# DeltaNet tasks: order edges behind the latest dense evacuation, scaling or substitution step

## The chip, cores and metric

The kernel runs on one core of one Trainium2 chip. The metric is device time in microseconds (us). The kernel before takes 1623.09 us, the median of 3 runs (1622.53 to 1624.87).

## What is computed

A trunk of two layers over 16 meta tokens and 512 tokens with 1024 channels: a forgetting-attention layer and a gated DeltaNet layer, each followed by a feed-forward block with a short causal convolution (FFN). The change concerns the DeltaNet layer alone. Cut to what matters, with 8 heads of 128 channels and chunks of 64 or 128 rows:

```
proj = h @ w_in                       # q, k, v, output gate, two gate scalars per head
q, k, v = silu(causal_dwconv(q, 4 taps)), ...    # then q and k are l2-normalised
g = cumsum of the log decay, beta = sigmoid(gate)
for each chunk:
    A = strictly lower part of beta * exp(g_i - g_j) * (k_i . k_j)
    T = inverse(I + A)
    u = T @ (beta * v - (beta * exp(g) * k) @ S)
    o = (exp(g) * q) @ S + (masked q k^T) @ u
    S = exp(g_last) * S + k_decayed^T @ u
out = rmsnorm(o) * gate @ w_out
```

## The kernel before

The sequence is worked on in two halves of 272 and 256 columns. The large products are made by `dense`: for one 128-channel tile of one half it issues 24 matmuls into one PSUM tile (`ps`, L339; the activations are split into a high part `xh` and a low part `xl`). The tile is then taken out of PSUM by VectorE (DVE). In the DeltaNet layer there are three such evacuations: `conv_tile` L778 (`ub`, DVE) with a scaling on ScalarE (ACT) at L785 and the remaining taps on DVE at L794; the output gate `og` L1547 (`oz`, DVE) with a tanh on ACT at L1549; and the output projection `part` L914 and L916 (`m`, DVE). Until `ub` or `oz` has been read, TensorE (PE) has no free PSUM tile and stops.

Beside the dense products run generator tasks for four groups (g0 to g3) of two heads each. A planner, the class `Flow`, keeps a clock of its own that advances with each matmul issued; `tick` lets a task take its next step when its wake time has passed, and the `yield` of a step says how long to wait (in us). The tasks that matter here:

- `decays` (L1100 to L1129): loads the decays of a head by DMA into `gcr` (L1114), and makes masked differences on DVE (L1123, tiles `Dm` and `ATQD`).
- `gram_k` (L1132 to L1161): products of keys on PE, their diagonal on DVE (L1144, L1145, tile `y`), a power on GpSimd (POOL, L1146, tile `rk`), then `rho` on DVE (L1147) and what follows from it (L1148 to L1157).
- `solve` (L1271 to L1374): the inverse. POOL does a substitution of 31 steps of two instructions (L1295, L1296) for each group; the result goes out and comes back by DMA into `Rc`; DVE transposes it into `Tc` (L1309); further products follow on PE (L1317 to L1370, tile `l`), with copies on DVE (L1327) and ACT (L1328).
- the meta-token inverse, whose products are L1220 on PE and whose copies are `Y` on DVE (L1245 to L1265), the scan over the chunks (L1380 to L1413 on PE, ACT and DVE: `VB`, `KD`, `U`, `S`), and the heads' output (`MO` with a power on POOL at L1466, `OU` on ACT at L1470, the transposition `t` on PE at L1476, `o` on DVE at L1484).

The order on PE is fixed by tokens that are stamped in the planner's order. On DVE, ACT and POOL there was no such rule: the tile scheduler sets the order of their instructions from its own estimate of when each is ready, and each engine then works strictly through its list. An instruction that waits for a DMA therefore holds all that stand behind it on its engine, an evacuation too.

Of the kernel before, what the change touches and what calls it, by code (L numbers as in the profile page):

```python
# [12 lines left out]
AF = mybir.ActivationFunctionType  # L13
ALU = mybir.AluOpType
# [18 lines left out]
T_GRAM = 4.5  # L33
# [12 lines left out]
T_POW = 2.4  # L46
# [67 lines left out]
def trunk(ctx, tc, h0, wflat, params, out):  # L114
    nc = tc.nc
# [25 lines left out]
    def phase(name):  # L141
        turn.clear()
        turn["kinds"] = KINDS[name]
# [81 lines left out]
    class Flow:  # L225
# [10 lines left out]

        def step(self, t):
            self.busy = True
            try:
                r = next(t["gen"])  # L240
            except StopIteration:
                self.tasks.remove(t)
                r = None
            self.busy = False
            t["cond"] = None
            if callable(r):
                t["cond"] = r
            elif r is not None:
                t["wake"] = self.now + r
# [14 lines left out]
        def until(self, cond):  # L264
            assert not self.busy
            while not cond():
                if not self.ready():
                    self.now += 0.5
                    continue
                t = min(self.ready(), key=lambda t: t["wake"])  # L270
                self.now = max(self.now, t["wake"])
                self.step(t)

    flow = Flow()

# [491 lines left out]
    def conv_tile(u, half, ft, taps, base, stride, pool, carry):  # L767
        n = HALF[half][1]
        c0 = taps - 1
        xh, xl, r = xk(half)  # L770
        ps = dense(u, half, xh, xl)
        with tc.high_priority(offset=300):
            ub = pool.tile([P, 275], F32, name="ub", tag="ub", bufs=3)
            if half == 0:
                nc.gpsimd.memset(ub[:, 0:c0], 0.0)
            else:
                nc.gpsimd.tensor_copy(ub[:, 0:c0], carry.pop(ft)[:, :c0])  # L777
            nc.vector.tensor_tensor(ub[:, c0:c0 + n], ps, r[:, :n], op=ALU.mult)  # L778
            if half == 0:
                c = pool.tile([P, 3], F32, name="cy", tag="cy", bufs=8)  # L780
                nc.gpsimd.tensor_copy(c[:, :c0], ub[:, n:n + c0])  # L781
                carry[ft] = c
            w = [prm[:, base + i * stride + ft:base + i * stride + ft + 1] for i in range(taps)]
            cv = tmp2("cv")[:, :n]
            nc.scalar.activation(cv, ub[:, c0:c0 + n], AF.Identity, scale=w[c0])  # L785
            tap = u - DN0 in DN_TAP
            if tap:
                t0 = tmp("cv0")[:, :n]
                if u - DN0 > 13:
                    nc.gpsimd.tensor_scalar(t0, ub[:, 0:n], w[0], None, op0=ALU.mult)  # L790
                else:
                    nc.scalar.activation(t0, ub[:, 0:n], AF.Copy, scale=w[0])
            for i in range(c0 - 1, 0 if tap else -1, -1):
                nc.vector.scalar_tensor_tensor(cv, ub[:, i:i + n], w[i], cv, op0=ALU.mult, op1=ALU.add)  # L794
            if tap:
                nc.gpsimd.tensor_tensor(cv, cv, t0, op=ALU.add)
        return cv
# [73 lines left out]
    def deltanet(layer, post, pre, wcx):  # L871
# [22 lines left out]
        def part(u, half, j, last):  # L894
            n = NT[half]
            if j == 0 and not last:
                drop(*X[half][:2])
                m[half] = take(half, "m", shape=[P, KT, n])
            if j == 0 and last:

                if half == 0:
                    HALF[0] = (CUT, NT[0])
                ssm[half] = SumSq(half)
            if j == 0:
                OHL[half] = split(half, 4 * last)
                if last:
                    drop(O[half])
            x = OHL[half]
            for sub in range(2):
                mt = 2 * j + sub  # L910
                ps = dense(u, half, lambda k: x[:, 0, k, :], lambda k: x[:, 1, k, :], 0, n, sub)
                mm = m[half][:, mt, :]
                if not last:
                    nc.vector.tensor_copy(mm, ps)  # L914
                    continue
                nc.vector.tensor_tensor(mm, mm, ps, op=ALU.add)  # L916
                ssm[half].add(mm)
                if mt == 4:
                    h[half] = take(half, "h", shape=[P, KT, n])
                    nc.gpsimd.dma_start(h[half][:], hd_[half][:, :, CUT if half == 0 else 0:])  # L920
            if j == 3:
                drop(x)
                if last:
                    boundary(half, m[half], ssm[half], post, pre)
                    drop(m[half])
# [4 lines left out]
        with ExitStack() as cx:  # L930
            flow.on = True
            dn_heads(layer, O, cx, part)
            flow.on = False
        phase("ffn")
        wide(wcx)

    def dn_heads(layer, O, cx, part):
# [108 lines left out]
        def group(g):  # L1046
# [84 lines left out]
            def gram_k(half):  # L1131
                s, n = HALF[half]  # L1132
                cs = slice(CI[half][0], CI[half][-1] + 1)
                w = len(CI[half])
# [3 lines left out]
                y, rk, rho, ab, ub, kd = (col(x) for x in ("y", "rk", "rho", "ab", "ub", "kd"))  # L1138
# [5 lines left out]
                        nc.vector.tensor_tensor_reduce(out=dg, in0=pgs[hl][:, i * 128:i * 128 + cn], in1=ident[:, 0:cn], scale=1.0, scalar=0.0, op0=ALU.mult, op1=ALU.add, accum_out=y[:, c, hl:hl + 1])  # L1144
                nc.vector.tensor_scalar(y[:, cs, :], y[:, cs, :], 0.25, EPS, op0=ALU.mult, op1=ALU.add)  # L1145
                nc.gpsimd.tensor_tensor(rk[:, cs, :], y[:, cs, :], mhalf[:, 0:w * NG].rearrange("p (c x) -> p c x", x=NG), op=ALU.pow)  # L1146
                nc.vector.tensor_tensor(rho[:, cs, :], y[:, cs, :], rk[:, cs, :], op=ALU.mult)  # L1147
                nc.vector.tensor_scalar(rk[:, cs, :], rk[:, cs, :], 0.5, None, op0=ALU.mult)  # L1148
                nc.vector.tensor_tensor(ub[:, cs, :], rk[:, cs, :], COL[:, cs, hs4], op=ALU.mult)
# [2 lines left out]
                for hl in range(NG):  # L1152
                    for i, c in enumerate(CI[half]):
                        cn = CH[c][1]
                        o = pgs[hl][:cn, i * 128:i * 128 + cn]
                        d, a = (st["QD"][:, hl * 4 + c - 1, :], st["AT"][:, hl * 4 + c - 1, :]) if c else (st["Dm"][:, hl, :], padded("N", 0)[hm(hl), hm(hl)])
                        nc.vector.scalar_tensor_tensor(a, o, ab[:cn, c, hl:hl + 1], d, op0=ALU.mult, op1=ALU.mult)  # L1157
                if half == 0:
                    nc.vector.tensor_copy(ub[32:64, 0, 0:1], ub[0:32, 0, 1:2])
                yield T_GRAM + 1.5  # L1160
                held["g"] = False  # L1161


# [106 lines left out]
            def solve():  # L1270
# [21 lines left out]
                for l in range(31):  # L1292
                    a, w = l // 4 + 1, 31 - l
                    t = PR[:, 0:a * w].rearrange("p (j i) -> p j i", i=w)
                    nc.gpsimd.tensor_tensor(t, R3[:, 0:a, l:l + 1].to_broadcast([P, a, w]), A3[:, l:l + 1, l + 1:32].to_broadcast([P, a, w]), op=ALU.mult)  # L1295
                    nc.gpsimd.tensor_tensor(R3[:, 0:a, l + 1:32], R3[:, 0:a, l + 1:32], t, op=ALU.subtract)  # L1296
                    yield T_STEP
                for r in range(4):
                    nc.sync.dma_start(dR[:, :, r, :], RB[32 * r:32 * r + 32, :].rearrange("p (j i) -> p j i", i=32))
# [240 lines left out]
        def og(u, half, hd):  # L1540
            c = slice(CUT if half == 0 else 0, HALF[half][1])
            n = c.stop - c.start
# [1 line left out]
            ps = dense(u, half, xh, xl, c.start, c.stop)  # L1544
            otile(half)
            z = tmp2("oz")[:, :n]
            nc.vector.tensor_tensor(z, ps, r[:, c], op=ALU.mult)  # L1547
            th = tmp2("ot")[:, :n]
            nc.scalar.activation(th, z, AF.Tanh, scale=0.5)  # L1549
            o = O[half][:, hd, c]  # L1550
            w = max(written.get((half, hd), 0) - c.start, 0)
            og_done.add((half, hd))
# [96 lines left out]
```

## Time and profile before

| | |
|---|---|
| median of 3 runs | 1623.09 us (1622.53 to 1624.87) |
| the profiled execution | 1624.94 us |
| its span, first to last instruction | 1623.0 us, mean granted TensorE clock 0.966 |
| DeltaNet stage in the span | about 791 to 1215 us |
| PE busy over the span | 1528.3 us (94%) |
| DVE, ACT, POOL busy | 1144.3, 800.0 and 456.2 us |

PE is the busiest engine. The table by stretches shows for each stretch of the span how long each engine was busy, and as PEclk the granted TensorE clock as a share of full speed (0.5 is the lower of its two levels, 1.2 GHz). The lists of waits name an instruction, what ended its wait, the total of these waits, their number and the longest. In a timeline an instruction stands with its start, its duration, and in brackets the idle time of its engine before it and what ended that.

### The profile page before, as it was taken

What the parts mean: (1) busy time and instruction counts of PE and PEld (TensorE: products, weight loads), DVE (VectorE), ACT (ScalarE), POOL (GpSimd) and SP (SyncE); (2) the same over time, 40 slices, a digit from 0 to 9 for tenths busy, and PEclk for the clock granted to TensorE, in tenths of its full rate; (3) what the DMA queues carried; (4) which work ended last, traced back from release to release, by engine and by line L of the source; (5) the groups of instructions that cost most, each with busy time, mean ns of one, the idle gap of its engine ahead of it and who ended that gap; (6) DMA issues with size and microseconds to landing.
All of it is one profiled execution on the core that took longest, in us unless ns stands there. A gap on an engine that the chain in (4) does not pass through costs nothing.

```text
span 1623.0 us, 32915 instructions
## 1 busy us (share of the span) xinstructions
PE 1528.3 (94%) x12462; PEld 1491.8 (92%) x12462; DVE 1144.3 (71%) x2760; ACT 800.0 (49%) x1849; POOL 456.2 (28%) x949
## 2 busy tenths in 40 slices
PE   8999999999999999999779798989898999999996
PEld 6999999899999999998679787988887999999996
DVE  7888888849964665665878765857477864765764
ACT  6777777735543432444463334545454543433441
POOL 6444443135200100114534555161043100100112
PEclk9999999999999999999799898999998999999998
DMA  5322322421323223222233331222231223323321
GB/s 172 100 80 73 86 73 86 132 79 53 105 84 99 92 81 103 92 83 79 93 108 81 76 83 41 63 72 61 78 113 57 80 84 100 93 90 94 100 68 53
DMA packets 66527, 139.55 MB, mean 86 GB/s; under 512 B 22808, under 2 KB 35512, under 8 KB 65984
## 3 DMA queue, kind: packets, MB, share of 16 engines
q1 hardware_dynamic: 65744, 135.08, 28.0%
q8 instruction: 98, 1.61, 0.4%
q0 software_dynamic: 480, 2.15, 0.4%
q14 instruction: 61, 0.50, 0.1%
q10 hardware_dynamic: 144, 0.22, 0.0%
HBM read 132.06 MB, written 5.36 MB: 85 GB/s over the span
## 4 chain that ended last, share of the span: by engine, by line
PE 74%; DVE 11%; POOL 5%; ACT 4%; DMA 3%; issue 3%; SPq 1%; POOLq 0%; DVEq 0%; ACTq 0%
PE ps L339 64%; POOL PR L1295 2%; POOL RB L1296 2%; DVE bt L438 1%; DVE w L310 1%; DVE h L439 1%; PE av L728 1%; DMA gcr<-gcd 1%; DVE cv L794 1%; PE pt L708 1%; DVE xl L405 1%; ACT w L303 1%; PE sc L676 1%; PE sc L677 1%; PE pt L696 1%
## 5 line engine op out<-in xcount | busy, mean ns | idle before, releaser
L339 PE MATMUL ps<-xh,w 128*128 128x256 f32 (+5 forms) x4928 | 974.6, 292 | 30.6 <-DVE ub L778 19.4
L339 PEld LDWEIGHTS ps<-xh,w 128*128 128x128 f32 (+2 forms) x4928 | 793.8, 192 | 37.7 <-DVE ub L778 21.6
L339 PE MATMUL ps<-xl,w 128*128 128x256 f32 (+5 forms) x2464 | 713.2, 290 | 10.8 <-DVE xl L405 10.8
L339 PEld LDWEIGHTS ps<-xl,w 128*128 128x128 f32 (+2 forms) x2464 | 473.9, 192 | 15.7 <-DVE xl L405 13.9
L303 ACT CAST w<-w 128x1024 fp32r<-128x1024 f32 (+2 forms) x218 | 223.3, 1025 | 158.9 <-PE ps L339 143.3
L310 DVE TENSOR_TENSOR w<-w,w 128x1024 fp32r<-128x1024 f32 (+3 forms) x183 | 221.6, 1211 | 112.1 <-ACT w L303 112.1
L794 DVE SCALAR_TENSOR_TENSOR cv<-ub,prm,cv 128x256 f32<-128x256 f32 (+2 forms) x494 | 241.8, 495 | 40.9 <-ACT cv L785 32.0
L339 PE MATMUL ps<-ah,w 128*128 128x256 f32 (+2 forms) x1408 | 265.0, 284 | 0.0
L339 PEld LDWEIGHTS ps<-ah,w 128*128 128x128 f32 x1408 | 221.5, 188 | 0.0
L339 PE MATMUL ps<-al,w 128*128 128x256 f32 (+2 forms) x704 | 199.1, 283 | 0.0
L785 ACT ACTIVATE cv<-ub,prm 128x256 f32<-128x256 f32 (+2 forms) x224 | 113.3, 510 | 150.8 <-DVE ub L778 150.6
L778 DVE TENSOR_TENSOR ub<-ps,r 128x256 f32<-128x256 f32 (+2 forms) x224 | 95.5, 429 | 86.7 <-PE ps L339 83.6
L380 POOL TENSOR_TENSOR ssq<-ssq,sq 128x256 f32<-128x256 f32 (+2 forms) x98 | 93.1, 954 | 147.5 <-ACT sq L379 145.3
L339 PEld LDWEIGHTS ps<-al,w 128*128 128x128 f32 x704 | 132.5, 188 | 0.0
L781 POOL COPY cy<-ub 128x2 f32<-128x2 f32 (+1 forms) x112 | 35.7, 322 | 295.7 <-DVE ub L778 295.0
L310 POOL TENSOR_TENSOR w<-w,w 128x512 fp32r<-128x512 f32 x70 | 93.6, 1357 | 63.5 <-ACT w L303 44.5
L777 POOL COPY ub<-cy 128x2 f32<-128x2 f32 (+1 forms) x112 | 31.7, 283 | 213.8 <-DVE cv L794 173.0
L816 ACT ACTIVATE gl<-cv 128x272 f32<-128x272 f32 (+2 forms) x88 | 36.7, 418 | 47.9 <-DVE cv L794 47.7
L841 DVE TENSOR_TENSOR m<-m,ps 128x256 f32<-128x256 f32 (+2 forms) x64 | 27.2, 424 | 41.5 <-PE ps L339 41.0
L1295 POOL TENSOR_TENSOR PR<-RB,AB 128x60 f32<-128x60 f32 (+24 forms) x124 | 44.6, 360 | 36.6 <-DMA AB<-dA 28.5
L339 PE MATMUL ps<-ohl,w 128*128 128x260 f32 (+1 forms) x384 | 51.7, 288 | 2.6 <-ACT ohl L887 1.0
L339 PEld LDWEIGHTS ps<-ohl,w 128*128 128x128 f32 x384 | 47.7, 190 | 4.1 <-ACT ohl L887 1.3
(325 smaller groups left out, 2175.3 us busy)
## 6 DMA issues: line engine op xcount, KB each, us to landing
w<-wflat SPq DMA_DIRECT2D x184, 512.0 KB, 3.5
w<-wflat SPq DMA_DIRECT2D x32, 448.0 KB, 3.3
cB<-cdram SPq DMA_DIRECT2D x16, 264.0 KB, 3.3
h<-h SPq DMA_DIRECT2D x8, 272.0 KB, 4.8
cB<-cdram SPq DMA_DIRECT2D x16, 136.0 KB, 3.0
h<-h SPq DMA_DIRECT2D x8, 256.0 KB, 4.7
AB<-dA SPq DMA_DIRECT2D x16, 128.0 KB, 2.9
out<-h SPq DMA_DIRECT2D x16, 128.0 KB, 1.8
```

Of the source, the lines that this page charges most:

```text
L303: nc.scalar.copy(wh, w32)
L310: eng.tensor_tensor(wl[:, c], w32[:, c], wh[:, c].bitcast(F32), op=ALU.subtract)
L339: tok(nc.tensor.matmul(o, w[:, a], r[:, c0:c1], start=(i == 0), stop=(i == tot - 1)))
L380: nc.gpsimd.tensor_tensor(self.acc[:, :n], self.acc[:, :n], sq[:, :n], op=ALU.add)
L777: nc.gpsimd.tensor_copy(ub[:, 0:c0], carry.pop(ft)[:, :c0])
L778: nc.vector.tensor_tensor(ub[:, c0:c0 + n], ps, r[:, :n], op=ALU.mult)
L781: nc.gpsimd.tensor_copy(c[:, :c0], ub[:, n:n + c0])
L785: nc.scalar.activation(cv, ub[:, c0:c0 + n], AF.Identity, scale=w[c0])
L794: nc.vector.scalar_tensor_tensor(cv, ub[:, i:i + n], w[i], cv, op0=ALU.mult, op1=ALU.add)
L816: nc.scalar.activation(g, cv, AF.Gelu_apprx_tanh)
L1295: nc.gpsimd.tensor_tensor(t, R3[:, 0:a, l:l + 1].to_broadcast([P, a, w]), A3[:, l:l + 1, l + 1:32].to_broadcast([P, a, w]), op=ALU.mult)
L1296: nc.gpsimd.tensor_tensor(R3[:, 0:a, l + 1:32], R3[:, 0:a, l + 1:32], t, op=ALU.subtract)
```

## The change

A dictionary `anchors` keeps for DVE, ACT and POOL the latest instruction of a kind: on DVE the latest evacuation (`ub`, `oz` or `m`), on ACT the latest scaling or tanh behind an evacuation, on POOL the latest subtraction of the substitution. Every step of a task is traced under `tc.issue_after(anchor)`, so that its instructions on that engine get an order edge behind that anchor. The edges are orders within an engine and add no instruction; the counts of instructions on each engine are the same. In `gram_k` a `yield T_POW` (2.4 us) is put behind the power, and its last `yield` falls from 6.0 to 3.5 us.

```diff
@@ -236,11 +236,14 @@
 
         def step(self, t):
             self.busy = True
-            try:
-                r = next(t["gen"])
-            except StopIteration:
-                self.tasks.remove(t)
-                r = None
+            with ExitStack() as es:
+                for i in anchors.values():
+                    es.enter_context(tc.issue_after(i))
+                try:
+                    r = next(t["gen"])
+                except StopIteration:
+                    self.tasks.remove(t)
+                    r = None
             self.busy = False
             t["cond"] = None
             if callable(r):
@@ -270,6 +273,14 @@
                 t = min(self.ready(), key=lambda t: t["wake"])
                 self.now = max(self.now, t["wake"])
                 self.step(t)
+
+    anchors = {}
+
+    def anchor(engine, inst):
+        if flow.on:
+            anchors[engine] = inst.ins
 
     flow = Flow()
 
@@ -775,14 +786,14 @@
                 nc.gpsimd.memset(ub[:, 0:c0], 0.0)
             else:
                 nc.gpsimd.tensor_copy(ub[:, 0:c0], carry.pop(ft)[:, :c0])
-            nc.vector.tensor_tensor(ub[:, c0:c0 + n], ps, r[:, :n], op=ALU.mult)
+            anchor("dve", nc.vector.tensor_tensor(ub[:, c0:c0 + n], ps, r[:, :n], op=ALU.mult))
             if half == 0:
                 c = pool.tile([P, 3], F32, name="cy", tag="cy", bufs=8)
                 nc.gpsimd.tensor_copy(c[:, :c0], ub[:, n:n + c0])
                 carry[ft] = c
             w = [prm[:, base + i * stride + ft:base + i * stride + ft + 1] for i in range(taps)]
             cv = tmp2("cv")[:, :n]
-            nc.scalar.activation(cv, ub[:, c0:c0 + n], AF.Identity, scale=w[c0])
+            anchor("act", nc.scalar.activation(cv, ub[:, c0:c0 + n], AF.Identity, scale=w[c0]))
             tap = u - DN0 in DN_TAP
             if tap:
                 t0 = tmp("cv0")[:, :n]
@@ -911,9 +922,9 @@
                 ps = dense(u, half, lambda k: x[:, 0, k, :], lambda k: x[:, 1, k, :], 0, n, sub)
                 mm = m[half][:, mt, :]
                 if not last:
-                    nc.vector.tensor_copy(mm, ps)
+                    anchor("dve", nc.vector.tensor_copy(mm, ps))
                     continue
-                nc.vector.tensor_tensor(mm, mm, ps, op=ALU.add)
+                anchor("dve", nc.vector.tensor_tensor(mm, mm, ps, op=ALU.add))
                 ssm[half].add(mm)
                 if mt == 4:
                     h[half] = take(half, "h", shape=[P, KT, n])
@@ -931,6 +942,7 @@
             flow.on = True
             dn_heads(layer, O, cx, part)
             flow.on = False
+            anchors.clear()
         phase("ffn")
         wide(wcx)
 
@@ -1144,6 +1156,7 @@
                         nc.vector.tensor_tensor_reduce(out=dg, in0=pgs[hl][:, i * 128:i * 128 + cn], in1=ident[:, 0:cn], scale=1.0, scalar=0.0, op0=ALU.mult, op1=ALU.add, accum_out=y[:, c, hl:hl + 1])
                 nc.vector.tensor_scalar(y[:, cs, :], y[:, cs, :], 0.25, EPS, op0=ALU.mult, op1=ALU.add)
                 nc.gpsimd.tensor_tensor(rk[:, cs, :], y[:, cs, :], mhalf[:, 0:w * NG].rearrange("p (c x) -> p c x", x=NG), op=ALU.pow)
+                yield T_POW
                 nc.vector.tensor_tensor(rho[:, cs, :], y[:, cs, :], rk[:, cs, :], op=ALU.mult)
                 nc.vector.tensor_scalar(rk[:, cs, :], rk[:, cs, :], 0.5, None, op0=ALU.mult)
                 nc.vector.tensor_tensor(ub[:, cs, :], rk[:, cs, :], COL[:, cs, hs4], op=ALU.mult)
@@ -1157,7 +1170,7 @@
                         nc.vector.scalar_tensor_tensor(a, o, ab[:cn, c, hl:hl + 1], d, op0=ALU.mult, op1=ALU.mult)
                 if half == 0:
                     nc.vector.tensor_copy(ub[32:64, 0, 0:1], ub[0:32, 0, 1:2])
-                yield T_GRAM + 1.5
+                yield T_GRAM - 1
                 held["g"] = False
 
 
@@ -1293,7 +1306,7 @@
                     a, w = l // 4 + 1, 31 - l
                     t = PR[:, 0:a * w].rearrange("p (j i) -> p j i", i=w)
                     nc.gpsimd.tensor_tensor(t, R3[:, 0:a, l:l + 1].to_broadcast([P, a, w]), A3[:, l:l + 1, l + 1:32].to_broadcast([P, a, w]), op=ALU.mult)
-                    nc.gpsimd.tensor_tensor(R3[:, 0:a, l + 1:32], R3[:, 0:a, l + 1:32], t, op=ALU.subtract)
+                    anchor("pool", nc.gpsimd.tensor_tensor(R3[:, 0:a, l + 1:32], R3[:, 0:a, l + 1:32], t, op=ALU.subtract))
                     yield T_STEP
                 for r in range(4):
                     nc.sync.dma_start(dR[:, :, r, :], RB[32 * r:32 * r + 32, :].rearrange("p (j i) -> p j i", i=32))
@@ -1544,9 +1557,9 @@
             ps = dense(u, half, xh, xl, c.start, c.stop)
             otile(half)
             z = tmp2("oz")[:, :n]
-            nc.vector.tensor_tensor(z, ps, r[:, c], op=ALU.mult)
+            anchor("dve", nc.vector.tensor_tensor(z, ps, r[:, c], op=ALU.mult))
             th = tmp2("ot")[:, :n]
-            nc.scalar.activation(th, z, AF.Tanh, scale=0.5)
+            anchor("act", nc.scalar.activation(th, z, AF.Tanh, scale=0.5))
             o = O[half][:, hd, c]
             w = max(written.get((half, hd), 0) - c.start, 0)
             og_done.add((half, hd))
```

(In the changed kernel the lines from L240 on have numbers that are higher by 3, those of `conv_tile` by 11, and those from L1147 on by 13.)

What moves on the engines. The order on PE of the dense matmuls stays. The 16 `MEMSET` rows of L959 and L1431 on DVE, which clear the tasks' tiles, leave the boundary between the FFN and DeltaNet stages, where they stood between the rows of L405, L438 and L439, and stand behind evacuations of the DeltaNet stage. The other moves show in three places.

First, DVE in the projections of the DeltaNet stage, where the decays of g1 (rows `Dm<-gcr` and `ATQD_11765<-gcr`) are made. `ub<-ps` is an evacuation. Before:

```order
L794 SCALAR_TENSOR_TENSOR cv<-ub,prm,cv 128x256
L1145 TENSOR_SCALAR y<-y 128x6
L1123 SCALAR_TENSOR_TENSOR Dm<-gcr,COL,dmask 16x16
L1123 SCALAR_TENSOR_TENSOR ATQD_11765<-gcr,COL,dmask 128x128 x2
L794 SCALAR_TENSOR_TENSOR cv<-ub,prm,cv 128x256
L1123 SCALAR_TENSOR_TENSOR Dm<-gcr,COL,dmask 16x16
L1123 SCALAR_TENSOR_TENSOR ATQD_11765<-gcr,COL,dmask 128x128 x2
L778 TENSOR_TENSOR ub<-ps,r 128x256
```

The same rows now:

```order
L805 SCALAR_TENSOR_TENSOR cv<-ub,prm,cv 128x272 x2
L789 TENSOR_TENSOR ub<-ps,r 128x256
L1135 SCALAR_TENSOR_TENSOR Dm<-gcr,COL,dmask 16x16
L1135 SCALAR_TENSOR_TENSOR ATQD_11765<-gcr,COL,dmask 128x128 x2
L1203 TENSOR_SCALAR eq<-g 128x6
L1135 SCALAR_TENSOR_TENSOR Dm<-gcr,COL,dmask 16x16
L1135 SCALAR_TENSOR_TENSOR ATQD_11765<-gcr,COL,dmask 128x128
```

They stood ahead of an evacuation, and now stand seven dense tiles later and directly behind one; the decays of g2 and g3 move later by three to five tiles.

Second, DVE where the result of g1's substitution is transposed (`Tc<-Rc`). Before:

```order
L1390 SCALAR_TENSOR_TENSOR VB<-s,COL,VB 128x128
L1309 STREAM_TRANSPOSE Tc<-Rc 128x256
L1547 TENSOR_TENSOR oz<-ps,r 128x256
L1327 COPY TM<-Tc 32x8x32
L1245 COPY Y_11485<-l 64x64
L310 TENSOR_TENSOR w<-w_13028,w 128x1024
```

The same place of the program and the place of the transposition now:

```order
L1258 COPY Y_11476<-l 64x64
L1403 SCALAR_TENSOR_TENSOR VB<-s,COL,VB 128x128 x2
L1560 TENSOR_TENSOR oz<-ps,r 128x256
L321 TENSOR_TENSOR w<-w_13389,w 128x1024
L1262 TENSOR_TENSOR Y_11478<-l,ident 64x64
L1567 SCALAR_TENSOR_TENSOR o_12676<-ot,oz 128x256
L789 TENSOR_TENSOR ub<-ps,r 128x272
L1322 STREAM_TRANSPOSE Tc<-Rc 128x256
L1266 TENSOR_TENSOR Y_11476<-l,Y_11478 64x64
```

The transposition now follows the copies of `Y` that it held up, four dense tiles later. For g0 it moves by two tiles, for g2 by seven (258 to 265, the dense tiles counted from the kernel's start) and for g3 by two (275 to 277), while PE's first use of it (L1317) stays behind dense tile 258 for g1, 268 for g2 and 278 for g3, and moves from 248 to 251 for g0.

Third, POOL in g0's substitution, where the power of g1's first half stands (`rk<-y,mhalf`). Before:

```order
L1295 TENSOR_TENSOR PR<-RB,AB 128x75
L1296 TENSOR_TENSOR RB<-RB,PR 128x5x15
L775 MEMSET ub 128x3
L1295 TENSOR_TENSOR PR<-RB,AB 128x70
L1146 TENSOR_TENSOR rk<-y,mhalf 128x6
L1296 TENSOR_TENSOR RB<-RB,PR 128x5x14
L781 COPY cy<-ub 128x3
```

The power's place now:

```order
L1308 TENSOR_TENSOR PR<-RB,AB 128x66
L1309 TENSOR_TENSOR RB<-RB,PR 128x6x11
L1158 TENSOR_TENSOR rk<-y,mhalf 128x6
L1308 TENSOR_TENSOR PR<-RB,AB 128x60
L1309 TENSOR_TENSOR RB<-RB,PR 128x6x10
```

It stays within the substitution, now between two whole steps; `rho`, which waits for it on DVE, stays ahead of the same evacuation.

## Rows read from the trace of the kernel before

**Rows 1.** The table by stretches, boundary and parts of the DeltaNet stage (start:end, length, then busy time).
```profile
core 0: us, PE busy (x) PEld busy (x) DVE busy (x) ACT busy (x) POOL busy (x), PEclk, DMA share, GB/s
760.00:780.00 20.00, 10.47 (x61) 7.27 (x59) 19.91 (x44) 9.92 (x21) 15.29 (x22) 0.74 0.43 154
...
840.00:1020.00 180.00, 153.53 (x1281) 147.78 (x1280) 126.75 (x437) 74.08 (x197) 93.42 (x266) 0.90 0.29 71
1020.00:1080.00 60.00, 59.74 (x583) 58.77 (x582) 46.82 (x138) 34.27 (x96) 25.62 (x67) 1.00 0.27 74
1080.00:1100.00 20.00, 13.43 (x87) 12.53 (x86) 8.90 (x27) 5.13 (x13) 5.27 (x23) 0.76 0.36 63
1120.00:1180.00 60.00, 54.05 (x453) 50.70 (x453) 32.36 (x86) 29.48 (x90) 6.13 (x8) 0.94 0.23 72
```

**Rows 2.** The list of waits of PE, 740 to 1225 us.
```profile
PE ps L339 <- DVE ub L778: 19.4, 8, 5.5
...
PE s L1395 <- ACT KD L1392: 7.1, 7, 2.1
...
PE t L1476 <- ACT OU L1470: 4.0, 3, 2.3
...
PE l L1359 <- DVE o L1484: 2.5, 1, 2.5
PE l L1220 <- DVE Y L1245: 2.5, 1, 2.5
PE l L1317 <- DVE Rm L1265: 1.9, 1, 1.9
```

**Rows 3.** The list of waits of DVE, 800 to 1200 us.
```profile
DVE Tc L1309 <- DMA Rc<-dR: 13.2, 3, 4.8
...
DVE rho L1147 <- POOL rk L1146: 9.5, 5, 3.5
```

**Rows 4.** The timeline of DVE at the boundary (start, duration, instruction).
```profile
767.27 0.17 DVE L959 MEMSET QDm<- 128x128 f32 x1
767.41 0.17 DVE L959 MEMSET Rm<- 128x128 f32 x1
```

**Rows 5.** The timeline of DVE at g1's decays, then of PE there.
```profile
849.64 0.22 DVE L1123 SCALAR_TENSOR_TENSOR Dm<-gcr,COL,dmask 16x16 f32<-16x16 f32 x1 [1.14 <-DMA gcr<-gcd]
...
851.38 0.40 DVE L778 TENSOR_TENSOR ub<-ps,r 128x256 f32<-128x256 f32 x1
...
851.84 0.58 PE L339 MATMUL ps<-xh,w 128*128 128x256 f32 x1 [3.01 <-DVE ub L778]
```

**Rows 6.** The table by stretches, the slices with a lower clock.
```profile
840.00:860.00 20.00, 16.92 (x126) 16.42 (x125) 15.52 (x60) 9.49 (x27) 5.58 (x10) 0.91 0.36 92
...
900.00:920.00 20.00, 15.94 (x109) 15.43 (x108) 15.86 (x58) 6.87 (x19) 10.74 (x36) 0.85 0.36 73
...
960.00:980.00 20.00, 17.51 (x124) 17.29 (x124) 11.28 (x30) 8.75 (x25) 8.96 (x28) 0.83 0.38 98
```

**Rows 7.** The timeline of DVE at the decays of g2.
```profile
914.74 0.22 DVE L1123 SCALAR_TENSOR_TENSOR Dm<-gcr,COL,dmask 16x16 f32<-16x16 f32 x1 [1.21 <-DMA gcr<-gcd]
```

**Rows 8.** The timeline at the transposition of g1, DVE, then PE.
```profile
966.88 0.45 DVE L1309 STREAM_TRANSPOSE Tc<-Rc 128x256 f32<-128x256 f32 x1 [4.05 <-DMA Rc<-dR]
...
968.01 0.69 PE L1220 MATMUL l<-Y,N 128*128 128x64 f32 x2 [2.49 <-DVE Y L1245]
```

**Rows 9.** The timeline at the transposition of g3, DVE, then PE.
```profile
1095.54 0.45 DVE L1309 STREAM_TRANSPOSE Tc<-Rc 128x256 f32<-128x256 f32 x1 [4.81 <-DMA Rc<-dR]
...
1096.86 1.22 PE L1401 MATMUL s<-U,KD 128*128 128x128 f32 x4 [3.90 <-ACT U L1397]
```

**Rows 10.** The timeline at a power inside g0's substitution, POOL, DVE, then PE.
```profile
895.22 1.34 POOL L1146 TENSOR_TENSOR rk<-y,mhalf 128x6 f32<-128x6 f32 x1
...
896.59 0.27 DVE L1147 TENSOR_TENSOR rho<-y,rk 128x6 f32<-128x6 f32 x1 [3.49 <-POOL rk L1146]
...
898.98 0.41 PE L339 MATMUL ps<-xh,w 128*128 128x256 f32 x1 [4.05 <-DVE ub L778]
```

## Prediction

> **What bounds the kernel now.** I read the table by stretches first, because the change acts in the DeltaNet stage alone [rows 1]. From 840 to 1020 us PE is busy for 153.53 of 180 us, at a granted clock of 0.90; from 1020 to 1080 us for 59.74 of 60 us, at 1.00. The same dense work can thus run almost without a gap, and the first stretch loses 26.5 us of idleness and some 18 us at the lower clock. Then I read what PE waits for [rows 2]. The largest entry is the evacuation `ub`, 19.4 us in 8 waits. But evacuations take only 0.40 us [rows 5], so the question is what stands ahead of them on DVE. The waits of DVE answer it [rows 3]: the transposition `Tc` waits 13.2 us in 3 waits for the DMA of `Rc`, `rho` waits 9.5 us for POOL. The timelines show the mechanism [rows 5, 8, 9]: an instruction of a task waits on DVE for a DMA, an evacuation or copy behind it is late, and PE stops, after which its clock is granted at half for a while. This is a bound by order, not by throughput: DVE is busy for 126.75 of the 180 us [rows 1].
>
> **The change part by part.** The sum is made against the profiled execution, 1624.94 us; the median is 1.85 us lower, and I subtract the same gains from the median.
>
> (1) Boundary. The 16 `MEMSET` rows follow each other at 0.14 us [rows 4], in a slice where DVE is busy for 19.91 of 20 us and PE for 10.47 [rows 1]. DVE is the bound there, so 16 x 0.14 = 2.2 us go. Behind evacuations of the stage I cost them at nothing, since DVE is idle there for 53 of 180 us; without that cover they cost 2.2 us again.
>
> (2) Decays of g1. `Dm` waits 1.14 us for its DMA, and with what follows it the evacuation starts at 851.38; PE waits 3.01 us [rows 5]. Without these rows DVE is free at 849.64 - 1.14 = 848.5 and has two rows of L794 left; I take 2.4 us of the 3.01. The slice has a clock of 0.91, which is 1.8 us lost [rows 6]. Together 4.2 us. The decays then come seven tiles later, behind an evacuation, when their DMA has long landed.
>
> (3) Decays of g2. The wait shown is 1.21 us [rows 7]; a second of the same kind, which lies between nothing and as much again, I take at 0.8. The slice's clock of 0.85 costs 3.0 us [rows 6], half of which I put to this place and half to the one in (7): 2.0 + 1.5 = 3.5 us.
>
> (4) Transposition of g0. PE waits 1.9 us at L1317 [rows 2]. The product now comes three tiles later. Three slices (this one, that of g1 and that of g2) show the clock of 0.83, which is 3.4 us each [rows 6]. 5.3 us.
>
> (5) Transposition of g1. DVE waits 4.05 us, the copy `Y` stands behind it, and PE waits 2.49 us [rows 8]. `Y` now stands ahead of `Tc`: 2.5 + 3.4 = 5.9 us.
>
> (6) Transposition of g2. PE waits 2.5 us at L1359 for an `o` that stands behind it on DVE [rows 2]. It moves by seven tiles: 2.5 + 3.4 = 5.9 us.
>
> (7) Transposition of g3 and the power in g0's substitution. The first holds PE for 3.90 us [rows 9], and with the same 3.4 us of clock is worth 7.3; but `Tc` moves by two tiles only and its use on PE stays one tile behind it, so I count half, 3.7 us. The second is not mended: POOL makes the power between substitution steps, `rho` waits 3.49 us for it, and PE 4.05 us behind the evacuation that follows [rows 10]. In the new order `rho` stays ahead of that evacuation, and PE arrives about 6 us earlier after (1) and (2), while g0's substitution starts about one tile later in PE's order. It may cost nothing more, or its whole price again (4.05 + 1.5 = 5.6); I take 3.0 us, near the middle, because POOL's chain also gains a part of the 6 us.
>
> Sum: 2.2 + 4.2 + 3.5 + 5.3 + 5.9 + 5.9 + 3.7 = 30.7 us, less 3.0 is 27.7 us.
>
> (8) What is late next. PE's order is fixed, so when it arrives earlier it meets the tasks that were just in time. The waits that the change leaves are those of the scan and of the heads' output: `KD` 7.1 us in 7 and `OU` 4.0 us in 3 [rows 2]. Their chains go through ACT, DVE and POOL, none of which becomes faster. The least is that they grow by nothing, the most that they take the 27.7 us back. I let them double, by 11.1 us, because PE's share of waiting in the later stretch of the scan, which has none of the removed waits, is 5.95 of 60 us [rows 1], against 26.5 of 180: a stage limited by its tasks still waits two thirds as much. The inserted `yield` in `gram_k` (2.4 us, with 2.5 us taken off the last one) I cost at nothing: it leaves `gram_k` 0.1 us shorter in the planner's clock.
>
> Net 27.7 - 11.1 = 16.6 us: 1624.94 becomes 1608.3, and the median of 1623.1 becomes **1606.5 us**. As a check from other rows: if 840 to 1020 and 1080 to 1100 us lost only what 1120 to 1180 us loses, (5.95 + 3.6 of clock) / 60 or 16% of 200 us, they would give back 55.9 - 31.8 = 24 us.
>
> **The clock as a point of doubt.** Of the 30.7 us of gains in (1) to (7), 15.2 are clock (1.8 + 1.5 + 3 x 3.4 + 1.7). The rows show it lower in the slices in which PE waited behind evacuations and copies [rows 5, 6, 8]. The Trainium skill says otherwise on the page "TensorE: Matmul & The Clock Gate", in the section "Loop structure matters more than you think": a copy out of PSUM on VectorE between iterations is marked there as not breaking PE's warmth. By the rows the gains stand at 30.7 us, by the page at 15.5. The trace disagrees with the page here.
>
> **Rivals.**
> - *All of it* (10%): the chains behind (8) move along, since DVE and POOL are freed as well, and (7) counts whole: 30.7 + 3.6 = 34.3 us, 1589 us. For it speaks the stretch from 1020 to 1080 us, with the same kind of work and no loss [rows 1]; against it the scan, which waits for its own results.
> - *Little* (10%): the new place of `Tc` is one tile ahead of its use, and chains of the solve now end late; the waits come back under the names of `l` tiles and `S`. Half or more of the net is gone again: 16.6 / 2 = 8 us or less, 1615 to 1620 us. For it speaks that PE's place for L1317 did not move for g1, g2 and g3; against it that `Tc` had waited there with tiles to spare.
> - *Nothing* (8%): the clock stays low in these slices, because shorter gaps are left that keep it there or because the gaps on DVE's account are not what lowers it. Then the 15.2 us of clock do not come, and 16.6 - 15.2 = 1.4 us are left: 1621.7 us. For it speaks that 1080 to 1100 us shows the lowest clock, 0.76, with several waits close together [rows 1]; against it that 1020 to 1080 us, without gaps, shows 1.00. The page named above would have it so.
> - *Slower* (10%): POOL becomes the place that holds the evacuations. The edges keep the powers behind the latest substitution step, and four of the eight powers stand within or close to a substitution. If each makes `rho` late as the one in [rows 10], that is 4 x (4.05 + 1.7) = 23 us against the 19.6 us that (1) to (8) give without the 3.0 of (7): 3.4 us slower, 1626.5 us. It decides from the point where the power ends about one dense tile (3 us) after `y`. Against it: `rho` waits for POOL only 9.5 us in all now, with one wait of 3.5 [rows 3].
> - That the edges change no order is excluded: the orders of DVE and POOL differ, as the three places above show.
>
> **How the numbers follow.** My forecast, a gain of 8 to 28 us with 16.6 the likeliest, has 62%. With *all* (10%) and *little* (10%) faster by over 0.2% (3.25 us, about what a measurement of this kernel can tell from no change) has 0.82, within 0.2% has 0.08, slower has 0.10. The range reaches down to 1592, which leaves out the outer half of *all* and a little of the forecast's edge, and up to 1624, which takes in *little* and *nothing* and leaves out *slower*. That leaves about 2 in 10 outside.
>
> **What would show it.** Right, if the changed profile has no `Tc <- Rc` and no `Dm <- gcr` worth naming among DVE's waits; if PE's wait for `ub` falls from 19.4 us to about 10 (the longest, 5.5 us, stands behind DVE's work on the gates, which is no task and stays, and the power's stays too); if the slices at 920, 960 and 1000 us show a clock near 1; and if `KD` and `OU` grow. The FFN and attention stages must keep their times. Wrong, if `rho <- rk` grows past 20 us, or if waits of PE for `l` and `s` products rise by more than 25 us: then the edges have only moved the lateness to the tasks.

## The result, and the profile after

The changed kernel took 1608.18 us, the median of 4 runs (1607.41 to 1613.27), against 1623.93 us before in the same comparison (4 runs). The ratio is 0.991, with a 95% interval of 0.9888 to 0.9933: faster by 15.7 us, where 16.6 were forecast. The kernel before differs a little from chip to chip (its medians below lie between 1620.5 and 1623.9 us), so the experiments are compared by their ratio to it.

The profiled execution took 1607.41 us with a span of 1605.5 us. The DeltaNet stage without its boundaries, from 800 us until the same dense product is reached, shows where the gain is. The table by stretches, kernel before:

```profile
800.00:1200.00 400.00, 355.22 (x3030) 343.59 (x3029) 271.72 (x803) 190.48 (x499) 154.30 (x405) 0.92 0.28 75
```

and the changed kernel:

```profile
800.00:1184.00 384.00, 346.14 (x3025) 333.91 (x3024) 271.18 (x820) 187.35 (x499) 155.60 (x407) 0.95 0.29 78
```

The stretch is 16 us shorter. PE's idle time falls from 44.8 to 37.9 us, by 6.9, and its busy time for the same matmuls (but for 5 of 3030) from 355.2 to 346.1 us, by 9.1. More than half of the gain is thus the clock, whose mean rises from 0.92 to 0.95. This compares one execution of each kernel: over the whole span the mean clock of the kernel before lies between 0.965 and 0.974 from run to run, that of the changed kernel between 0.971 and 0.978.

The lists of waits of the changed kernel name the wait, its total, number and longest. PE, 740 to 1215 us:

```profile
PE ps L350 <- DVE ub L789: 16.4, 11, 6.1
...
PE t L1489 <- ACT OU L1483: 6.3, 3, 4.4
PE g L1182 <- DVE ATQD L1170: 3.7, 1, 3.7
PE s L1408 <- ACT KD L1405: 3.1, 5, 1.1
```

PE's waits for `ub` fall by 3.0 us only, from 19.4 in 8 to 16.4 in 11. DVE, 790 to 1215 us:

```profile
DVE rho L1160 <- POOL rk L1158: 11.8, 2, 6.6
...
DVE ATQD L1135 <- DMA gcr<-gcd: 0.7, 1, 0.7
```

Against [rows 2, 3] the waits of `Tc` for `Rc` (13.2 us) are gone from DVE, and with them PE's waits at L1317 and L1359, while the longest at L1220 is 1.3 us now, of 2.5; one of 0.7 us is left for `gcr`. What has grown is `rho`'s wait for POOL, from 9.5 us in five to 11.8 in two. `KD` fell from 7.1 to 3.1 us, `OU` rose from 4.0 to 6.3, and a wait of 3.7 us at L1182, a product of keys, for `gram_k`'s `ATQD` is new.

ACT's list, which the prediction did not use, has a wait for a DMA that is longer in total than DVE's for `Rc` and `gcr` together (19.8 us): that for `eg`, the decays that the products with queries load. Kernel before, 790 to 1215 us:

```profile
ACT eg L1203 <- DMA eg<-gcd: 25.9, 13, 6.2
```

In the changed kernel this line is gone.

The timelines say what the two waits of `rho` are. Changed kernel, POOL, DVE and PE at the place of [rows 10]:

```profile
888.16 0.16 DVE L1157 TENSOR_SCALAR y<-y 128x6 f32<-128x6 f32 x1
...
894.34 1.33 POOL L1158 TENSOR_TENSOR rk<-y,mhalf 128x6 f32<-128x6 f32 x1
...
895.70 0.27 DVE L1160 TENSOR_TENSOR rho<-y,rk 128x6 f32<-128x6 f32 x1 [5.21 <-POOL rk L1158]
...
897.64 0.58 PE L350 MATMUL ps<-xh,w 128*128 128x256 f32 x1 [6.06 <-DVE ub L789]
```

`y` is ready at 888.3 us, but POOL works on substitution steps until 894.3; `rho` and the evacuation behind it wait, and PE's 4.05 us have become 6.06. The same happens with g2's power. There `rho` waited before as well, but no wait of PE stood behind it. Kernel before, DVE and POOL:

```profile
941.47 0.17 DVE L1145 TENSOR_SCALAR y<-y 128x6 f32<-128x6 f32 x1
...
944.94 1.35 POOL L1146 TENSOR_TENSOR rk<-y,mhalf 128x6 f32<-128x6 f32 x1
...
946.32 0.27 DVE L1147 TENSOR_TENSOR rho<-y,rk 128x6 f32<-128x6 f32 x1 [2.97 <-POOL rk L1146]
```

Changed kernel:

```profile
946.45 1.34 POOL L1158 TENSOR_TENSOR rk<-y,mhalf 128x6 f32<-128x6 f32 x1
...
947.83 0.25 DVE L1160 TENSOR_TENSOR rho<-y,rk 128x6 f32<-128x6 f32 x1 [6.56 <-POOL rk L1158]
...
949.51 1.23 PE L1182 MATMUL g<-hd 128*128 128x128 f32 x4 [3.75 <-DVE ATQD L1170]
```

The other power, `MO` of the heads' output, holds PE too; it stands among steps of g2's substitution:

```profile
983.09 0.70 POOL L1479 TENSOR_TENSOR MO<-MO,mhalf 128x2 f32<-128x2 f32 x1
...
983.82 0.37 ACT L1483 ACTIVATE OU<-o,MO 128x128 f32<-128x128 f32 x1 [4.81 <-POOL MO L1479]
...
984.25 0.86 PE L1489 MATMUL t<-ident,OU 128*128 128x128 f32 x2 [4.38 <-ACT OU L1483]
```

### The profile page after: what moved, and what is told of

It reads as the page before. It is cut to its first block, busy times and chain, and to the rows that moved or that the text cites. A ratio compares the mean times of both kernels' runs of the same rounds, so it can differ in the third digit from the quotient of the medians.

```text
span 1605.5 us, 32924 instructions
## 1 busy us (share of the span) xinstructions
PE 1520.5 (95%) x12462; PEld 1481.8 (92%) x12462; DVE 1142.7 (71%) x2760; ACT 797.0 (50%) x1849; POOL 455.4 (28%) x949
## 4 chain that ended last, share of the span: by engine, by line
PE 77%; DVE 11%; POOL 4%; ACT 3%; issue 3%; DMA 2%; SPq 1%; POOLq 0%; DVEq 0%; ACTq 0%
PE ps L350 66%; DVE w L321 1%; DVE cv L805 1%; PE av L739 1%; DVE bt L449 1%; DVE h L450 1%; POOL RB L1309 1%; POOL PR L1308 1%; ACT w L314 1%; PE pt L719 1%; DVE xl L416 1%; PE sc L687 1%; DMA w<-wflat 1%; PE sc L688 1%; PE g L1182 1%
## 5 line engine op out<-in xcount | busy, mean ns | idle before, releaser
L350 PE MATMUL ps<-xh,w 128*128 128x256 f32 (+5 forms) x4928 | 969.4, 291 | 26.5 <-DVE ub L789 16.4
L827 ACT ACTIVATE gl<-cv 128x272 f32<-128x272 f32 (+2 forms) x88 | 36.7, 418 | 47.9 <-DVE cv L805 47.6
```

What stands on the lines that cost most here:

```text
L350: tok(nc.tensor.matmul(o, w[:, a], r[:, c0:c1], start=(i == 0), stop=(i == tot - 1)))
L827: nc.scalar.activation(g, cv, AF.Gelu_apprx_tanh)
```

## The experiments

The theory after the result: tasks' instructions on DVE stood ahead of evacuations, and the edges take them away; what comes next late is a power on POOL that stands behind substitution steps. Rivals: the edges on the other engines carry the gain; the `yield`s do; or the places of DVE add up otherwise than the prediction has them. No run changes the attention and FFN stages; up to 767 us and from 1232 us on the profiles agree within 2.5 us with that of the kernel before.

**Which engine's edges.** In `anchor`, only the named engine is recorded:

```diff
-        if flow.on:
+        if flow.on and engine in ('dve',):
```

> The change with its edges on VectorE alone (ScalarE and GpSimd get none). Theory (the gain comes from tasks' VectorE instructions that no longer stand ahead of evacuations): the transposition Tc keeps its places of the changed kernel, and the time is that of the change within 4 us, 1604 to 1612 us. Rival (the edges on ScalarE and GpSimd carry half of it or more): 1616 us or more.

1612.14 us, 0.9938 (0.9921 to 0.9956).

```diff
-        if flow.on:
+        if flow.on and engine != "dve":
```

> The change with its edges on ScalarE and GpSimd alone. Theory (VectorE carries it): within 4 us of before, 1620 to 1628 us, and VectorE's waits of Tc for Rc stay near 13 us. Rival (half of the gain is here): 1612 to 1616 us.

1617.71 us, 0.9972 (0.9960 to 0.9984). DVE's edges give about 10 us; those on ACT and POOL, with the `yield`s, 4 to 5 us of their own, more than expected, while `Tc` still waits 11.3 us for `Rc`. What these edges do take away is ACT's wait for `eg`, 25.9 us before; 790 to 1215 us:

```profile
ACT eg L1216 <- DMA eg<-gcd: 0.5, 1, 0.5
```

With DVE's edges alone 21.1 us of it are left. That this wait is what the 4 to 5 us come from was not tried apart. The theory holds for the larger part only. The change was timed a second time on another chip:

> The changed kernel itself, beside the three below on one chip. Theory: 0.991 of before, 1606 to 1610 us. Nothing to tell apart; the others are compared with it.

1610.79 us, 0.9933 (0.9919 to 0.9946), just outside the expectation. Its two ratios, 0.9910 and 0.9933, overlap; the edges on DVE alone reach the second.

**The `yield`s.** The change with the two `yield`s as before:

```diff
-                yield T_POW
 ...
-                yield T_GRAM - 1
+                yield T_GRAM + 1.5
```

> The change with the two yields of gram_k as before (the edges alone). Theory (the yields shift the planner's clock by 0.1 us and are worth nothing): within 3 us of the change, 1605 to 1611. Rival (the yield behind the power is what parts rho from it and carries a third of the gain): 1613 or more.

1611.54 us, 0.9938 (0.9915 to 0.9961). This is half a us above the theory's range and not told apart from the change's 0.9933. The rival's third of the gain is not there against that value; against the other one, 0.9910, it cannot be excluded. The long wait for `rk` stays, 10.1 us in two.

**One place at a time.** In these the step of a task sets no edge, the `yield`s are as before, and only one kind of instruction gets the edge behind the latest evacuation:

```diff
+    def behind():
+        es = ExitStack()
+        if flow.on and "dve" in anchors:
+            es.enter_context(tc.issue_after(anchors["dve"]))
+        return es
```

The transpositions:

```diff
-                nc.vector.transpose(Tc[...], Rc[...])
+                with behind():
+                    nc.vector.transpose(Tc[...], Rc[...])
```

> The kernel before with an edge on the four transpositions Tc alone. Theory (terms 4 to 7 of the prediction are the largest part): PE's waits at L1317, L1220 and L1359 go, 1624 falls by 10 to 16 us to 1608 to 1614. Rival (the lateness only moves to the solve's own products): a gain under 5 us, above 1619.

1619.81 us, 0.9985 (0.9975 to 0.9994): 1.8 us, the rival's number. The waits of PE at L1317 and L1359 did go, that at L1220 fell to 0.5 us, and `Tc`'s for `Rc` went from DVE's list. Where the time went shows in three places of this kernel (the lengths of the stretches stand in the table further down). First the heads' output, POOL, ACT and PE:

```profile
988.16 0.70 POOL L1482 TENSOR_TENSOR MO<-MO,mhalf 128x2 f32<-128x2 f32 x1
...
988.90 0.37 ACT L1486 ACTIVATE OU<-o,MO 128x128 f32<-128x128 f32 x1 [6.64 <-POOL MO L1482]
...
989.32 0.47 PE L1492 MATMUL t<-ident,OU 128*128 128x128 f32 x1 [6.52 <-ACT OU L1486]
```

and in ACT's list of waits, 790 to 1215 us:

```profile
ACT OU L1486 <- POOL MO L1482: 21.1, 10, 6.9
```

Before, the same line reads 11.3 us in 6. PE comes earlier to the scan, finds the heads' output unfinished, because `MO`'s power stands behind steps of g2's substitution on POOL, and waits 6.52 us where it waited 2.3. This takes back what g2's place was to give, and not what g0's and g1's places had won before it. Second, g3's place, ACT and PE:

```profile
1094.70 0.80 ACT L1218 ACTIVATE eg<-eg 128x256 f32<-128x256 f32 x2 [7.07 <-DMA eg<-gcd]
...
1097.50 0.75 PE L1411 MATMUL s<-VB,ATQD 128*128 128x128 f32 x2 [2.24 <-ACT KD L1408]
```

PE no longer waits 3.90 us for `U`, but `KD` now stands on ACT behind an `eg` that waits 7.07 us for its DMA, and PE waits for `KD`. Third, the last products of g3's solve, where PE now waits 0.64 and 1.42 us (under 0.3 us each before): here the lateness did move to the solve, as the rival has it.

The masked differences of the decays:

```diff
-                        nc.vector.scalar_tensor_tensor(d, gcr[...], ...)
+                        with behind():
+                            nc.vector.scalar_tensor_tensor(d, gcr[...], ...)
```

> The kernel before with an edge on the masked differences of the decays alone (terms 2 and 3 of the prediction, 7.7 us, next-late waits not counted). Theory: 4 to 8 us faster, 1616 to 1620 us. Rival (the time is given back at the power in g0's substitution, which holds the evacuation all the same): within 2 us of before.

1611.55 us, 0.9931 (0.9915 to 0.9948): 10 us, more than the 7.7 of its terms, and the whole of what DVE's edges give. Its waits, DVE, 790 to 1215 us:

```profile
DVE rho L1163 <- POOL rk L1162: 13.8, 4, 5.2
...
DVE Tc L1325 <- DMA Rc<-dR: 6.6, 4, 4.9
...
DVE ATQD L1139 <- DMA gcr<-gcd: 0.3, 1, 0.3
```

`gcr` is gone but for 0.3 us, and half of `Tc`'s waiting as well, without an edge on `Tc`: the scheduler ordered other rows anew too, and g2's transposition stands two evacuations later. Both places together:

> The kernel before with edges on the transpositions and the masked differences of the decays alone. Theory (the places add up as in the prediction, less next-late waits): 3 to 6 us faster than the decays alone (0.993 of before), 0.990 or less. Rival (the two recover the same waits, since what is late next on GpSimd holds both): 0.992 to 0.995.

1614.11 us, 0.9955 (0.9942 to 0.9968): the edge on `Tc` adds nothing to that on the decays. `OU` waits for `MO` 24.1 us in 11 here.

The table has the lengths of eight stretches in us. Each is bounded by the starts of the same two evacuations on DVE in every kernel, and is named by their times in the kernel before. It compares single executions, whose totals differ from the medians by some us, and the tasks' products on PE move between stretches (up to 33 matmuls, from the fourth to the fifth).

| stretch (kernel before) | before | change | `Tc` alone | decays alone | both |
|---|---|---|---|---|---|
| 834.9 to 876.9, decays of g1 | 42.0 | 36.7 | 42.5 | 37.0 | 37.0 |
| 876.9 to 898.5, power of [rows 10] | 21.6 | 26.0 | 20.5 | 26.5 | 26.6 |
| 898.5 to 982.1, decays of g2, `Tc` of g0 and g1 | 83.6 | 74.9 | 77.8 | 77.7 | 73.2 |
| 982.1 to 1009.7, `Tc` of g2 | 27.6 | 26.5 | 26.9 | 22.7 | 26.5 |
| 1009.7 to 1080.8 | 71.1 | 77.3 | 73.0 | 71.6 | 73.2 |
| 1080.8 to 1106.6, `Tc` of g3 | 25.8 | 15.6 | 25.2 | 25.2 | 23.4 |
| 1106.6 to 1132.3, last products of g3's solve | 25.7 | 27.3 | 29.4 | 25.8 | 29.6 |
| 1132.3 to 1231.7 | 99.4 | 95.4 | 95.5 | 97.0 | 95.6 |

In the first two rows the rival of the decays run is right: what g1's decays give, 5.0 us, is given back at the power. Its gain comes from the next two rows. By the table both places together are no better than the decays alone because the edge on `Tc` wins 4.5 us in the third row and loses 3.8 in the fourth and 3.8 in the seventh. The largest single gain of the change, 10.2 us at g3's place, comes in none of these runs. Kernel before, then changed:

```profile
1080.80:1106.60 25.80, 19.23 (x133) 18.33 (x133) 12.74 (x38) 9.96 (x30) 6.45 (x26) 0.80 0.32 67
...
1075.90:1091.50 15.60, 15.60 (x136) 15.54 (x134) 12.12 (x34) 9.59 (x29) 4.25 (x16) 1.00 0.40 102
```

The stretch is 16.9 us long in the second profile of the change and 18.2 with DVE's edges alone. So it needs DVE's edges on other rows of the tasks as well; on which was not tried apart.

The `MEMSET` rows alone:

```diff
-                nc.vector.memset(zeroed[name, i][:], 0.0)
+                with behind():
+                    nc.vector.memset(zeroed[name, i][:], 0.0)
 ...
-                    nc.vector.memset(x[:], 0.0)
+                    with behind():
+                        nc.vector.memset(x[:], 0.0)
```

> The kernel before with an edge on the MEMSET rows alone (term 1 of the prediction: 2.2 us). Theory: 1 to 3 us faster than before. Rival (VectorE's other rows at the boundary stretch beside GpSimd and take the room): within 1 us of before.

1619.25 us, 0.9989 (0.9978 to 1.0000): 1.3 us by the medians. The sign is likely, the size within the theory and near the rival's limit. From the last evacuation of the FFN stage to the first of the DeltaNet stage it is 23.2 us here, 23.1 in the change and 24.2 before.

**What is late next.** The change, with the powers as anchors on POOL, so that a substitution step traced later stands behind them:

```diff
-                nc.gpsimd.tensor_tensor(rk[...], y[...], mhalf[...], op=ALU.pow)
+                anchor("pool", nc.gpsimd.tensor_tensor(rk[...], y[...], mhalf[...], op=ALU.pow))
```

> The change, with the power rk of gram_k also an anchor on GpSimd, so that later substitution steps stand behind it (it stands after 9 steps instead of 17 in g0's substitution, after 34 instead of 52 at the next). Theory (the power behind substitution steps is what holds rho, the evacuations and PE: 6.06 + 3.75 us of waits and 5.1 of clock in the change's trace): VectorE's wait of rho for rk falls from 11.8 us to under 4, and the time is 5 to 11 us below the change (1608), 1597 to 1603. Rival (the power only changes places with the substitution, whose result is then late at the transposition): within 2 us of the change, with waits of Tc for Rc back.

1606.42 us, 0.9908 (0.9893 to 0.9923). `rho`'s wait for `rk` is gone from DVE's list, but by its ratio the time is only 0 to 4 us below the change (0.9910 and 0.9933), and `Tc` waits for `Rc` again, 6.6 us in three: the rival is right about half. Beside the change without its `yield`s on the same chip (1611.54) it is 5.1 us faster, with intervals that overlap a little. With `MO` too:

```diff
-                nc.gpsimd.tensor_tensor(mo, mo, mhalf[:, 0:nh], op=ALU.pow)
+                anchor("pool", nc.gpsimd.tensor_tensor(mo, mo, mhalf[:, 0:nh], op=ALU.pow))
```

> As the run before, with the power MO of the heads' output an anchor too. Theory: PE's wait at L1489 for OU (6.3 us, the longest 4.4, and about 3 of clock behind it) falls under 3 us, 2 to 7 us below the run before. Rival (GpSimd then waits for MO's sums, which come late from ScalarE, and holds the substitution): no faster than the run before.

1602.20 us, 0.9883 (0.9868 to 0.9898): 4.2 us below the run before, as the theory had it, though in this profile one wait for `OU` of 5.2 us is left, so the theory's figure for that wait failed. The same kernel beside the change, on one chip:

> The version with both powers as anchors. Theory (powers behind substitution steps cost the change some 6 us net): 4 to 8 us below the change. Rival (the difference seen was one of chips): within 2 us of it.

1605.47 us, 0.9897 (0.9883 to 0.9912), 5.3 us below the change, whose interval (0.9919 to 0.9946) lies wholly above. At the place of [rows 10] it reads, DVE, POOL and PE:

```profile
887.36 0.16 DVE L1157 TENSOR_SCALAR y<-y 128x6 f32<-128x6 f32 x1
...
887.65 1.35 POOL L1158 TENSOR_TENSOR rk<-y,mhalf 128x6 f32<-128x6 f32 x1
...
889.65 0.27 DVE L1160 TENSOR_TENSOR rho<-y,rk 128x6 f32<-128x6 f32 x1
...
891.57 0.39 PE L350 MATMUL ps<-xh,w 128*128 128x256 f32 x1 [0.78 <-DVE ub L789]
```

The power follows `y` at once, and PE's 6.06 us are 0.78. The bill is in DVE's list, 790 to 1215 us:

```profile
DVE Tc L1322 <- DMA Rc<-dR: 9.0, 4, 3.1
```

**The gates.** The version with both anchors, and the second half of `gates` made a task:

```diff
+            def rest():
+                nc.vector.tensor_scalar(z[R], z[R], prm[...], None, op0=ALU.add)
+                yield 0.6
...
+                flow.spawn(columns(), 4)
+
+            flow.spawn(rest(), 0.6)
```

> The version with both anchors, and the second half of the gates as a task with its own steps, so that its VectorE work stands behind evacuations as well. Theory (a row that is no task holds the evacuation at 822 us just the same: 5.2 us and 3.4 of clock): that wait of PE falls under 1.5 us, and the time is 4 to 9 us below the run before. Rival (the gates end later, the decays wait for them, and the later stage gives it back): within 2 us of the run before.

1604.17 us, 0.9887 (0.9875 to 0.9900), not told apart from the run before, and the wait did not move. DVE, then PE:

```profile
823.01 1.75 DVE L1018 SCALAR_TENSOR_TENSOR gt<-gt 8x528 f32<-8x528 f32 x1
824.79 1.15 DVE L1021 SCALAR_TENSOR_TENSOR gt<-gt 8x528 f32<-8x528 f32 x1
825.92 0.17 DVE L1023 MEMSET gt<- 8x128 f32 x1
826.12 0.49 DVE L805 SCALAR_TENSOR_TENSOR cv<-ub,prm,cv 128x256 f32<-128x256 f32 x1
826.52 0.44 DVE L789 TENSOR_TENSOR ub<-ps,r 128x272 f32<-128x272 f32 x1
...
827.01 0.58 PE L350 MATMUL ps<-xh,w 128*128 128x256 f32 x1 [5.25 <-DVE ub L789]
```

The theory is wrong. The rival's number is met, but not for its reason, since the wait is still there. An edge behind the latest evacuation leaves a row free to stand ahead of the next one, and these do, in the same order as before.

## Why the prediction was right, and where it was not

The time, the direction and the net were right. The terms behind the net were largely wrong, and that they cancelled to within 1 us (16.6 forecast, 15.7 measured) is luck.

**The mechanism** was right in its main part. Task rows on DVE that wait for a DMA held evacuations, and with them gone the stage is 16 us shorter (shown by the DVE edges and by the decays alone).

**(1) Boundary**, 2.2 us: alone it gave 1.3 us, uncertain. Right in sign, somewhat too large. DVE is still busy for 19.91 of 20 us from 760 to 780 us in the changed kernel.

**(2), (3) Decays**, 7.7 us: alone 10 us. By the table g1's place gave 5.0 us, about as priced (4.2), and lost them at the power; the rest came with g2's decays and where the scheduler moved g2's transposition along, which I had not priced.

**(4) to (7) Transpositions**, 20.8 us: alone 1.8 us, and nothing on top of the decays. This is the step that failed. For g0 I misread the wait:

```profile
918.94 0.44 DVE L1309 STREAM_TRANSPOSE Tc<-Rc 128x256 f32<-128x256 f32 x1
...
927.69 0.33 DVE L1265 TENSOR_TENSOR Rm<-Y,l 16x16 f32<-16x16 f32 x2
...
928.17 0.23 PE L1317 MATMUL l<-Tc,ATQD 32*32 32x32 f32 x1 [1.88 <-DVE Rm L1265]
```

`Tc` of g0 waited for no DMA and was done nine us earlier; PE waited for `Rm` of the meta-token inverse. For all four I priced each wait as time won and left what it uncovers to (8). The waits did go. Alone, the places of g0 and g1, with the stretch around them, kept 5.8 us of the 11.2 priced; `MO` at g2's place and `eg` on ACT at g3's left 0.7 of 5.9 and 0.6 of 3.7; and the stretches behind each of these two lost 1.9 and 3.7 us. A wait at the head of a chain that feeds the scan is worth what the scan's other inputs have to spare, not its own length. In the change, where every step of a task has its edges, g3's place gave 10.2 us instead of 3.7, and g2's 1.1 instead of 5.9.

**(7) The power**: I charged 3.0 us for its growth. In the change PE's wait grew by 2.0 us at that place and came up once more at g2 (3.75 us at PE); the stretch of [rows 10] is 4.4 us longer. The condition of the *slower* rival, a power that ends more than about 3 us after `y`, was met in these two places (7.4 and 8.5 us), not in four. It was met in the same two before the change too (5.3 and 4.7 us), so it did not tell the two kernels apart. It cost part of the gain, not the whole.

**(8) What is late next**: forecast 11.1 us for `KD` and `OU` doubling. `KD` halved instead; the cost came as `OU` (from 4.0 to 6.3 us) and `rho`, both behind POOL's powers, and in the two stretches behind g2's and g3's places, which are 6.2 and 1.6 us longer. The amount made up for part of the error in (4) to (7); the place was wrong in half. That POOL holds it is shown for these powers by the version with both anchors, which is 5.3 us faster.

**The signs** came out mixed. `Tc` and `gcr` left DVE's list and `OU` grew, as written, and the slices at 920, 960 and 1000 us show a clock of 0.95, 0.92 and 0.94 (that at 980 us fell to 0.74); `KD` did not grow, and PE's wait for `ub` fell to 16.4 us, not to about 10, because the power's share of it grew by 2.0 us and several short waits are left.

**The clock**: of the forecast gross gain half was clock, and in the stage 9.1 of 16 us came as shorter busy time of the same matmuls. The rival that no clock comes back (*nothing*) is out. The page of the Trainium skill "TensorE: Matmul & The Clock Gate", section "Loop structure matters more than you think", marks a copy out of PSUM by DVE as not breaking PE's warmth, in an example whose next matmuls follow immediately. To say that the trace disagrees with it was too much: here they did not follow. PE waited 6.06 us for such a copy in the changed kernel, and the clock behind that wait was 0.50.

**The gates**: I wrote that their wait stays because they are no task. It stays, but the run with the gates as a task shows that this is not the reason.

The edges on ACT and POOL were costed at nothing and are worth 4 to 5 us alone, with the `yield`s; how much of this remains beside DVE's could not be told from these runs. The prediction looked for rows that wait for a DMA on DVE only, and ACT's `eg` waited longer than any of them.

## What to carry to other kernels

Where engines work strictly through a list that an estimate made, look for an instruction that waits for a DMA ahead of one that frees PSUM, and set it behind by an edge; then look at once for the next in-order list (here POOL's substitution), since several waits removed can be worth far less than their sum, and look on every engine for rows that wait for a DMA, not only on the one that holds PSUM. Price such a change by stretches and by what is late next, not by adding waits; a single place, tried alone, may give most of it, in part because the scheduler then orders other rows anew. An edge orders a row behind what has come, and not ahead of or behind what comes next: where a burst of work is to give way to the next evacuation, that evacuation has to be named.

## What the runs showed of the hardware

Half of the gain was not idle time but clock. Behind the wait of 6.06 us in the changed kernel the granted clock is at its lower level (0.50), and some us later at the upper one again (1.00). Table by stretches:

```profile
897.60:899.00 1.40, 1.36 (x6) 1.36 (x7) 1.33 (x7) 0.32 (x1) 1.24 (x4) 0.50 0.00 0
903.00:905.00 2.00, 1.81 (x16) 1.57 (x15) 1.94 (x10) 0.00 (x0) 1.77 (x7) 1.00 0.00 0
```

In this stage PE's busy time for the same matmuls differs by 9.1 us between the two kernels. The POOL power on six numbers per partition takes 1.33 us, more than four times the median substitution row (0.30 us in the changed kernel). One power in the wrong place of the list thus costs little itself, and `rho` waits up to 6.56 us for it by what stands ahead of it.
